# A two-block transformer on one core: the first matrix of each MLP as seven half-size products

## The chip, the cores and the metric

The kernel runs on one core of a Trainium2 chip. The metric is the device time of one execution in microseconds. TensorE multiplies matrices into PSUM, VectorE and ScalarE work elementwise, GpSimd does a few elementwise instructions, and SyncE (SP) issues all loads and stores.

## The reference

A sequence of 512 positions with 1024 features goes through three blocks: attention with an MLP, gated linear attention (GLA) with an MLP, and a hybrid mixer with a convolutional feed-forward. The part at hand is the MLP, which appears twice:

```python
def sq_relu_mlp(h, w_in, w_out):          # w_in 1024 x 4096, w_out 4096 x 1024
    return jnp.square(jax.nn.relu(h @ w_in)) @ w_out
...
for i in range(DEPTH):                    # DEPTH = 2
    ...
    h = h + sq_relu_mlp(rmsnorm(h, norm_mlp[i]), mlp_w_in[i], mlp_w_out[i])
```

All inputs are float32. The second reference block starts from a modulation, `mod = silu(c) @ w_ada + b_ada`, that depends on neither h nor x; the kernel computes it beside other work.

## The kernel before

Activations lie transposed: h is eight tiles of 128 features x 512 positions. A product keeps float32 precision with three matmuls in TensorE's faster float32r form: every operand x is split into a part xh rounded to float32r and a remainder xl = x - xh, and W x becomes Wh xh + Wh xl + Wl xh. ScalarE makes the rounded part (`hi`, line 456), VectorE the remainder (`lo`, line 459). `weights` (line 468) loads 128 x 1024 numbers of weights (512 KB) into a page w and splits them into wh and wl. `gemm` (line 478) then multiplies one such block into one PSUM bank: eight tiles k of 128 input features, three matmuls each, 24 matmuls of 512 columns.

`mlp` (line 803) first splits h times a gain into xs (`gained`, line 565). It goes through four groups g. In a group, eight blocks of the first matrix give eight tiles of 128 hidden features; each is multiplied with the norm's row rb after a maximum with 0 (VectorE), squared (ScalarE) and split into u. Then `residual` (line 758) runs the eight blocks of the second matrix that take this u, and VectorE adds each to h[n]. In the last group of the second MLP `halves` (line 972) does so with 256 columns at a time, so that the norm of the first 256 positions can start early. The modulation, `adaln` (line 764), is a generator: each `next(side)` in `mlp` lets it issue one more load of 512 KB (tile aw) and one multiply-add over 128 x 1024 on VectorE (tile acc).

`first` (line 990) opens the mixer and the feed-forward: it takes several blocks of weights at once, multiplies all of them with the first 256 positions, and then with the second, so that the second half of xs may come later. `ffn` (line 1284) calls it with seven blocks. `rope` (line 607) rotates queries and keys with four VectorE instructions; the attention calls it ten times, the mixer five times.

Nothing is issued in the order of the program text. `Plan` (line 95) records every instruction, then walks through them with a cost for each and, at each step, gives the engine that is free first its earliest instruction of the text that is ready. Tiles live in pages of five kinds (`PAGES`, line 421: bank, small, raw, half, full); an instruction that needs a page waits until one comes free, and it may not take a page that an earlier tile will need. `CAPS` limits some tags further. The result is one fixed order per engine.

Of the kernel before, what the change touches and what calls it, by code (L numbers as in the profile page):

```python
# [8 lines left out]
F = mybir.dt.float32  # L9
R = mybir.dt.float32r  # L10
I32 = mybir.dt.int32
U8 = mybir.dt.uint8
AF = mybir.ActivationFunctionType
OP = mybir.AluOpType
# [5 lines left out]
KT = 8  # L20
# [74 lines left out]
class Plan:  # L95
# [17 lines left out]
    def pages(self, kind, count):  # L113
        self.kinds[kind] = count
# [303 lines left out]
NCOL = _col_layout()  # L418


PAGES = {"bank": 8, "small": 96, "raw": 3, "half": 62, "full": 16}
CAPS = {"aw": 3, "acc": 2, "pth": 3, "ptl": 3, "wh": 4, "wl": 4, "qe": 3}
LASTING = ("cols", "ident", "hb", "g12", "mod", "w1024", "w256", "ones", "raw", "x2m", "fw", "ev", "blk", "part", "part", "bf", "k6", "fx", "fe", "rs")


class Net:
# [7 lines left out]
    def t(self, tag, cap, shape=(128, S), dt=F):  # L434
        size = math.prod(shape[1:]) * SIZE[dt]
        if tag in LASTING:
            return self.plan.lasting(tag, shape, dt)
        kind = "raw" if tag == "w" else next(k for k, b in (("small", 32), ("half", 2048), ("full", 4096)) if size <= b)
        return self.plan.tile(kind, tag, CAPS.get(tag), shape, dt)

    def g(self, shape=(128, S), dt=F):
# [8 lines left out]
    def bank(self, tag, shape=(128, S)):  # L450
        return self.plan.tile("bank", tag + "b", CAPS.get(tag + "b"), shape, F)

    def mm(self, out, lhsT, rhs, start, stop):
        self.nc.tensor.matmul(out, lhsT, rhs, start=start, stop=stop)

    def hi(self, out, x):
        self.nc.scalar.activation(out, x, AF.Copy)
# [30 lines left out]
    def gemm_nat(self, srcs, xs, n, bank="acc"):  # L488
        ws = []
        for src, kt in srcs:  # L490
            wh, wl = self.weights(src, (kt, n))
            ws += [(wh[:, k], wl[:, k]) for k in range(kt)]
        for i in range(4):
            ps = self.bank(bank)
            s = slice(i * 128, i * 128 + 128)
            for k, (xh, xl) in enumerate(xs):
                wh, wl = ws[k]
                self.mm(ps[:, :n], xh[:, s], wh, k == 0, False)
                self.mm(ps[:, :n], xh[:, s], wl, False, False)
                self.mm(ps[:, :n], xl[:, s], wh, False, k == len(xs) - 1)  # L500
            yield i, ps[:, :n]

    def rsqrt(self, x, n):
        nc = self.nc
# [102 lines left out]
    def rope(self, z, cs, sn, a=None):  # L607
        nc = self.nc
        sh, a = self.g(), self.g() if a is None else a
        nc.vector.stream_shuffle(sh, z, [j ^ 16 for j in range(32)])  # L610
        nc.vector.tensor_tensor(a, z, cs, op=OP.mult)
        nc.vector.tensor_tensor(sh, sh, sn, op=OP.mult)
        nc.vector.tensor_tensor(a, a, sh, op=OP.add)
        return a

    def keys(self, kn, e):
# [185 lines left out]

    def mlp(self, l, side=iter(()), after=None):
        nc, d, h = self.nc, self.d, self.h
        xs = self.gained(h, lambda k: self.col(f"nmlp{l}", k))
        rb = None
        for g in range(4):
            u = []
            for j in range(8):
                ps = self.gemm(d[f"w1_{l}"][g * 8 + j, 0], xs)  # L810
                if rb is None:
                    rb = self.row(self.rnorm(h, self.w1024)[0])
                next(side, None)
                t = self.g()
                nc.vector.scalar_tensor_tensor(t, ps, 0.0, rb, op0=OP.max, op1=OP.mult)
                nc.scalar.activation(t, t, AF.Square)
                u.append(self.split(t))
            if l == 0 or g < 3:
                self.residual(d[f"w2_{l}"], u, g, side)
            else:  # L820
                def evac(n, c, ps):
                    nc.vector.tensor_add(h[n][:, c], h[n][:, c], ps)
                    after(n, c)
                yield from self.halves(lambda n: d["w2_1"][n, 3], u, evac)

    def gla(self):
        nc, d, h = self.nc, self.d, self.h
# [183 lines left out]
    def mlp_norm2(self):  # L1011

        nc, h = self.nc, self.h
        gf = lambda k: self.col("fin", k)
        xs = [(self.t("xh", 8, dt=R), self.t("xl", 8, dt=R)) for _ in range(KT)]
        r1b, r12b = self.t("row", 2), self.t("row", 2)
        acc = [None]

        def squares(k, c):
            sq = self.big(dt=F)  # L1020
            nc.scalar.activation(sq[:, :256], h[k][:, c], AF.Square)
            nc.scalar.activation(sq[:, 256:], h[k][:, c], AF.Square, scale=gf(k))
            if k > 0:
                nc.vector.tensor_add(sq, acc[0], sq)
            acc[0] = sq

        for hf, c in self.mlp(1, after=squares):

            m, v = self.means(acc[0], self.w1024), self.small(4)
            nc.vector.tensor_scalar(v[:, :2], m[:, :2], EPS, None, op0=OP.add)  # L1030
            nc.vector.scalar_tensor_tensor(v[:, 2:], v[:, :2], EPS, m[:, 2:], op0=OP.mult, op1=OP.add)
            r = self.rsqrt(v, 4)
            self.row(r[:, 2:], r12b[:, c])
            self.row(r[:, :2], r1b[:, c])
        for hf in range(2):
            self.modulated(h, lambda k: self.g12[:, k:k + 1], 0, r12b, xs, slice(256 * hf, 256 * hf + 256))
        return xs, r1b
# [237 lines left out]
                (nc.vector if b == 2 else nc.gpsimd).tensor_tensor(m[n], m[n], x, op=OP.add)  # L1275

    def mlp0(self):
        side = self.adaln()
        for _ in self.mlp(0, side):
            pass  # L1280
        for _ in side:
            pass

    def ffn(self, xs):
        nc, d, h = self.nc, self.d, self.h
        ups = (0, 22, 1, 23, 2, 24, 3)
        pre = dict(zip(ups, self.first([d["wup"][j, 0] for j in ups], xs)))
        up = lambda j: pre.pop(j) if j in pre else self.gemm(d["wup"][j, 0], xs)
        y = [None] * KT
        for g, (j0, j1) in enumerate(((0, 8), (8, 16), (16, 22))):  # L1290
            u = []
            for j in range(j0, j1):
                a = up(j)
                c = self.g()
# [8 lines left out]
            for n in range(KT):  # L1303
                ps = self.gemm(d[f"wdn{g}"][n, 0], u)
# [5 lines left out]
        ps, sq, z = [None], [None], [None] * KT  # L1310
# [16 lines left out]
        for hf, c in self.halves(lambda n: d["wdn2"][n, 0], u, evac):  # L1327
            v = self.small(2)
            nc.vector.tensor_scalar(v, ps[0][:, :2], EPS, None, op0=OP.add)
            rb = self.bcast(self.rsqrt(v, 2))  # L1330
            for k in range(KT):
                x = y[k][:, c]
# [32 lines left out]
def _pack(w, kt):  # L1365
    k, n = w.shape
    return np.ascontiguousarray(w.reshape(k // (128 * kt), kt, 128, n // 128, 128).transpose(3, 0, 2, 1, 4)
                                ).reshape(n // 128, k // (128 * kt), 128, kt * 128)


def _nat(w, kt):
    k, n = w.shape
    return np.ascontiguousarray(w.reshape(k // (128 * kt), kt, 128, n).transpose(0, 2, 1, 3)).reshape(k // (128 * kt), 128, kt * n)


def _layout(a):
    a = {k: np.asarray(v) for k, v in a.items()}
    o = {}
# [3 lines left out]
    def put(name, v):  # L1382
        v = np.asarray(v).reshape(-1, 128).T
        cols[:, COLS[name]:COLS[name] + v.shape[1]] = v
# [11 lines left out]
    w = a["attn_w_qkv"][0]  # L1396
# [2 lines left out]
    o["wv"] = _nat(w[:, 1280:], 4)  # L1399
    o["wo"] = _pack(a["attn_w_o"][0], 8)  # L1400
    for l in range(2):
        o[f"w1_{l}"] = _pack(a["mlp_w_in"][l], 8)
        o[f"w2_{l}"] = _pack(a["mlp_w_out"][l], 8)
    w = a["gla_w_in"][0]
    o["wgq"] = _pack(w[:, :512], 8)
# [10 lines left out]
    j, c = np.arange(128)[:, None] % 64, np.arange(64)[None]  # L1416
# [63 lines left out]
```

## Time and profile before

| | |
|---|---|
| median of 3 runs | 1984.63 us (1984.07 to 1986.68) |
| profiled execution | 1984.77 us |
| its span | 1982.7 us |
| matmuls | 10389 |

The span runs from the first to the last instruction in the trace. Busy times are shares of it; matmuls overlap each other in the trace, so that a row's duration is longer than the time until the next one starts. In the trace all instructions carry the line of the recorder's `emit` (L352), so they are told apart by tile names and shapes.

### The profile page before, as it was taken

Reading aid. Unit: us, or ns where it says so; the run is one execution under the profiler, and the core shown is the slowest. Engines: PE = TensorE matmul, PEld = TensorE weight load, DVE = VectorE, ACT = ScalarE, POOL = GpSimd, SP = SyncE. Lnnn points to the kernel's source line nnn. Section 1 sums busy time; section 2 is a strip of 40 time slices with the busy share of each in tenths; the row PEclk is TensorE's granted clock in tenths of the full one; section 3 lists DMA queues with packets and bytes.
Section 4 is the critical chain, followed back from the end, with each engine's and each line's share of the span. In section 5 each row is a group of like instructions: output and inputs, shape, how many; then the busy total and the mean of one; then the engine's idle time right before and its main releaser. Section 6 shows DMA issues by size and latency. Waiting matters only on the chain.

```text
span 1982.7 us, 26560 instructions
## 1 busy us (share of the span) xinstructions
PE 1952.0 (98%) x10389; PEld 1654.6 (83%) x10389; DVE 1255.1 (63%) x2252; ACT 869.2 (44%) x1413; POOL 66.8 (3%) x110
## 2 busy tenths in 40 slices
PE   9899999999999999999999999999999999999997
PEld 8787788888889888888888899887888998888887
DVE  7999865746456677653434368899654685244346
ACT  6777642423346333442323255765443554233234
POOL 0000000000000001000000000100110000000001
PEclk9999999999999999999999999999999999999998
DMA  4012445745331222222323343231333423333322
GB/s 164 22 33 82 153 148 163 241 148 181 107 111 54 65 73 87 96 87 95 97 94 96 107 149 114 74 96 43 128 117 96 149 86 118 96 96 96 93 72 91
DMA packets 63628, 208.99 MB, mean 105 GB/s; under 512 B 7312, under 2 KB 10896, under 8 KB 63504
## 3 DMA queue, kind: packets, MB, share of 16 engines
q1 hardware_dynamic: 63504, 207.31, 32.7%
q8 instruction: 81, 1.33, 0.3%
q14 instruction: 43, 0.35, 0.1%
HBM read 203.08 MB, written 4.19 MB: 105 GB/s over the span
## 4 chain that ended last, share of the span: by engine, by line
PE 59%; DVE 1%; issue 0%; ACT 0%; POOL 0%
PE accb L352 50%; PE mb L352 3%; PE Sb L352 2%; PE ptb L352 2%; PE ob L352 1%; DVE big L352 1%; DVE c L352 0%; POOL ko L352 0%; ACT g L352 0%; ACT h L352 0%; DVE p L352 0%
## 5 line engine op out<-in xcount | busy, mean ns | idle before, releaser
L352 ACT ACTIVATE wh<-w 128x1024 fp32r<-128x1024 f32 (+2 forms) x337 | 346.3, 1030 | 730.7 <-PE accb L352 595.2
L352 DVE TENSOR_TENSOR wl<-w,wh 128x1024 fp32r<-128x1024 f32 (+2 forms) x336 | 399.3, 1190 | 274.9 <-ACT wh L352 195.4
L352 PE MATMUL accb<-big,wh 128*128 128x512 f32 (+1 forms) x2112 | 569.7, 357 | 0.0
L352 PE MATMUL accb<-xh,wh 128*128 128x512 f32 (+1 forms) x1344 | 524.5, 391 | 1.1 <-ACT wh L352 0.9
L352 PE MATMUL accb<-xl,wh 128*128 128x512 f32 (+1 forms) x1344 | 524.5, 390 | 0.0
L352 PE MATMUL accb<-xh,wl 128*128 128x512 f32 (+1 forms) x1344 | 523.4, 390 | 0.0
L352 PEld LDWEIGHTS accb<-big,wh 128*128 128x128 f32 x2112 | 373.1, 188 | 60.9 <-DVE big L352 0.2
L352 PE MATMUL accb<-big,wl 128*128 128x512 f32 (+1 forms) x1056 | 375.2, 356 | 0.0
L352 PEld LDWEIGHTS accb<-xh,wh 128*128 128x128 f32 x1344 | 253.2, 188 | 54.6 <-ACT wh L352 1.6
L352 PEld LDWEIGHTS accb<-xh,wl 128*128 128x128 f32 x1344 | 253.2, 188 | 53.0
L352 PEld LDWEIGHTS accb<-xl,wh 128*128 128x128 f32 x1344 | 253.3, 188 | 52.5 <-DVE xl L352 0.2
L352 PEld LDWEIGHTS accb<-big,wl 128*128 128x128 f32 x1056 | 198.7, 188 | 30.5
L352 DVE TENSOR_TENSOR h<-h,accb 128x512 f32<-128x512 f32 (+1 forms) x88 | 55.8, 635 | 109.4 <-PE accb L352 109.0
L352 DVE SCALAR_TENSOR_TENSOR g<-accb,row 128x512 f32<-128x512 f32 x64 | 44.0, 688 | 97.9 <-PE accb L352 93.6
L352 ACT ACTIVATE g<-g 128x512 f32<-128x512 f32 (+1 forms) x112 | 69.3, 629 | 74.9 <-DVE g L352 74.8
L352 DVE TENSOR_TENSOR big<-g,big 128x512 fp32r<-128x512 f32 (+2 forms) x124 | 81.8, 662 | 21.4 <-ACT big L352 21.1
L352 ACT ACTIVATE big<-g 128x512 fp32r<-128x512 f32 (+2 forms) x134 | 82.0, 613 | 29.9 <-DVE g L352 27.1
L352 DVE SCALAR_TENSOR_TENSOR acc<-aw,c,acc 128x1024 f32<-128x1024 f32 x42 | 53.8, 1281 | 24.8 <-DMA aw<-wada 24.6
L352 PE MATMUL ptb<-ident,p 128*128 128x128 f32 x376 | 61.2, 282 | 8.3 <-ACT p L352 4.6
L352 DVE TENSOR_TENSOR ptl<-ptb,pth 128x512 fp32r<-128x512 f32 (+2 forms) x112 | 64.4, 597 | 3.4 <-ACT pth L352 3.0
L352 PE MATMUL Sb<-big,q 128*128 128x512 f32 (+2 forms) x248 | 64.2, 379 | 2.1 <-ACT g L352 1.2
L352 PEld LDWEIGHTS ptb<-ident,p 128*128 128x128 f32 x376 | 45.6, 145 | 19.7 <-ACT p L352 12.1
(234 smaller groups left out, 2196.7 us busy)
## 6 DMA issues: line engine op xcount, KB each, us to landing
w<-w SPq DMA_DIRECT2D x136, 512.0 KB, 3.5
aw<-wada SPq DMA_DIRECT2D x48, 512.0 KB, 4.2
w<-wup SPq DMA_DIRECT2D x44, 512.0 KB, 3.5
w<-wzg SPq DMA_DIRECT2D x24, 512.0 KB, 3.5
w<-wout SPq DMA_DIRECT2D x16, 512.0 KB, 3.6
w<-wdn SPq DMA_DIRECT2D x16, 512.0 KB, 3.5
w<-wdn SPq DMA_DIRECT2D x16, 384.0 KB, 3.1
w<-wq SPq DMA_DIRECT2D x8, 512.0 KB, 4.5
```

The costliest lines, as they stand in the source:

```text
L352: getattr(getattr(self.nc, op.engine), op.name)(*map(real, op.args), **{k: real(v) for k, v in op.kwargs.items()})
```

## The change

The first matrix of each MLP is stored in quadrants of 256 x 512 (`_quads`). For a 2 x 2 split of weights (outputs by inputs) and of h (inputs by positions), `quad` forms seven products instead of eight, each of half the outputs, half the inputs and half the positions, in the Strassen-Winograd form. `spread` forms the sums of h once per MLP: seven right-hand sides with four tiles of 256 columns each, split like every operand. The sums of weights are three subtractions and an add of 128 x 1024 on VectorE per quad, before the split. Products 1, 6, 5 and 3 accumulate in one bank, with copies taken on ScalarE on the way (`kept`); products 7 and 4 share another, product 2 has its own. Two quads make a group's eight u tiles. The second matrix of group g - 1 is issued between the products of group g, one or two blocks at each `yield`; the first group has none between. The modulation now advances only at second-matrix blocks, so it reaches into the second MLP.

Pages change too: raw from 3 to 6 (it now holds the modulation's loads as well), half from 62 to 66, full from 16 to 11; the cap on acc goes. `first` in the feed-forward takes five blocks instead of seven. In `rope` two of the four VectorE instructions go to GpSimd.

```diff
-PAGES = {"bank": 8, "small": 96, "raw": 3, "half": 62, "full": 16}
-CAPS = {"aw": 3, "acc": 2, "pth": 3, "ptl": 3, "wh": 4, "wl": 4, "qe": 3}
+PAGES = {"bank": 8, "small": 96, "raw": 6, "half": 66, "full": 11}
+CAPS = {"aw": 2, "pth": 3, "ptl": 3, "wh": 4, "wl": 4, "qe": 3}
...
-        kind = "raw" if tag == "w" else next(k for k, b in (("small", 32), ("half", 2048), ("full", 4096)) if size <= b)
+        kind = "raw" if tag in ("w", "aw") else next(k for k, b in (("small", 32), ("half", 2048), ("full", 4096)) if size <= b)
...
+    def put(self, X, i, p, x):
+        xh, xl = self.pages(R), self.pages(R)
+        self.hi(xh, x)
+        self.lo(xl, x, xh)
+        X[p][2 * i:2 * i + 2] = [(xh[:, j], xl[:, j]) for j in range(2)]
+
+    def sums(self, X, i, B):
+
+        sub = lambda x, y: self.nc.vector.tensor_tensor(z := self.pages(), x, y, op=OP.subtract) or z
+        (b11, b12), (b21, b22) = B
+        t1, t3 = sub(b12, b11), sub(b22, b12)
+        t2 = sub(b22, t1)
+        t4 = sub(b21, t2)
+        for p, x in ((6, t2), (7, t3), (5, t1), (3, b22), (4, t4)):
+            self.put(X, i, p, x)
+
+    def spread(self, h, gain):
+
+        X, Bs = self.seven(), []
+        for i in range(2):
+            B = [[self.pages() for _ in range(2)] for _ in range(2)]
+            for r in range(2):
+                for c in range(2):
+                    for j in range(2):
+                        k = 4 * r + 2 * i + j
+                        self.nc.scalar.activation(B[r][c][:, j], h[k][:, c * 256:c * 256 + 256], AF.Copy, scale=gain(k))
+            Bs.append(B)
+            self.put(X, i, 1, B[0][0])
+        for i in range(2):
+            self.put(X, i, 2, Bs[i][1][0])
+        for i in range(2):
+            self.sums(X, i, Bs[i])
+        return X
+
+    def quad(self, src, X, sink):
+
+        nc = self.nc
+        A = {}
+        for r, i in ((0, 0), (0, 1), (1, 1), (1, 0)):
+            A[r, i] = self.t("w", 3, (128, 1024))
+            nc.sync.dma_start(A[r, i], src[2 * r + i])
+
+        def product(ps, x, p, start):
+            wh, wl = (self.t(a, 3, (128, 1024), R) for a in ("wh", "wl"))
+            self.hi(wh, x)
+            self.lo(wl, x, wh)
+            wh, wl = (a.rearrange("p (j k n) -> p j k n", j=2, k=4) for a in (wh, wl))
+            for n in range(8):
+                j, k = n // 2 % 2, n // 4 * 2 + n % 2
+                (xh, xl), o = X[p][k], ps[:, j]
+                self.mm(o, wh[:, j, k], xh, start and n == 0, False, skip_group_check=True)
+                self.mm(o, wh[:, j, k], xl, False, False, skip_group_check=True)
+                self.mm(o, wl[:, j, k], xh, False, n in (5, 7), skip_group_check=True)
+
+        def kept(ps):
+            z = self.pages()
+            nc.scalar.activation(z, ps, AF.Copy)
+            return z
+
+        sub = lambda z, x, y: nc.vector.tensor_tensor(z, x, y, op=OP.subtract)
+        a, b, c = (self.bank("acc", (128, 2, 256)) for _ in range(3))
+        product(a, A[0, 0], 1, True)
+        p1 = kept(a)
+        product(b, A[0, 1], 2, True)
+        sink(0, 0, b, p1)
+        yield
+        s1 = self.t("w", 3, (128, 1024))
+        nc.vector.tensor_add(s1, A[1, 0], A[1, 1])
+        sub(A[1, 0], A[0, 0], A[1, 0])
+        sub(A[0, 0], s1, A[0, 0])
+        product(a, A[0, 0], 6, False)
+        t6 = kept(a)
+        product(c, A[1, 0], 7, True)
+        yield
+        product(a, s1, 5, False)
+        t5 = kept(a)
+        sink(1, 1, c, t5)
+        yield
+        sub(A[0, 1], A[0, 1], A[0, 0])
+        product(a, A[0, 1], 3, False)
+        sink(0, 1, a, None)
+        product(c, A[1, 1], 4, False)
+        sink(1, 0, c, t6)
+        yield
...
-        nc.vector.tensor_tensor(sh, sh, sn, op=OP.mult)
-        nc.vector.tensor_tensor(a, a, sh, op=OP.add)
+        nc.gpsimd.tensor_tensor(sh, sh, sn, op=OP.mult)
+        nc.gpsimd.tensor_tensor(a, a, sh, op=OP.add)
...
     def mlp(self, l, side=iter(()), after=None):
         nc, d, h = self.nc, self.d, self.h
-        xs = self.gained(h, lambda k: self.col(f"nmlp{l}", k))
-        rb = None
+        X = self.spread(h, lambda k: self.col(f"nmlp{l}", k))
+        rb = self.row(self.rnorm(h, self.w1024)[0])
+
+        def hidden(g):
+
+            u = [None] * 8
+            for i in range(2):
+                T = [self.t("t", 3, (128, 2, 512)) for _ in range(2)]
+                left = [2, 2]
+
+                def sink(r, c, ps, x):
+                    t = T[r][:, :, c * 256:c * 256 + 256]
+                    if x is not None:
+                        nc.vector.tensor_add(t, ps, x)
+                        ps = t
+                    nc.vector.scalar_tensor_tensor(t, ps, 0.0, rb[:, None, c * 256:c * 256 + 256].to_broadcast([128, 2, 256]),
+                                                   op0=OP.max, op1=OP.mult)
+                    nc.scalar.activation(t, t, AF.Square)
+                    left[r] -= 1
+                    if not left[r]:
+                        for j in range(2):
+                            u[4 * r + 2 * i + j] = self.split(T[r][:, j])
+                for _ in self.quad(d[f"w1s_{l}"][g, i], X, sink):
+                    yield u
+
+        u = None
         for g in range(4):
...
+            out = [(w, n) for n, w in enumerate([d[f"w2_{l}"][n, g - 1] for n in range(KT)])] if g else []
+            for step, v in enumerate(hidden(g)):
+                for _ in range((1, 1, 2, 1, 1, 1, 1, 0)[step]):
+                    if out:
+                        w, n = out.pop(0)
+                        next(side, None)
+                        nc.vector.tensor_add(h[n], h[n], self.gemm(w, u))
+            u = v
+        if l == 0:
+            self.residual(d["w2_0"], u, 3, side)
...
-        for hf, c in self.mlp(1, after=squares):
+        for hf, c in self.mlp(1, self.modulation, squares):
...
-        ups = (0, 22, 1, 23, 2, 24, 3)
+        ups = (0, 22, 1, 23, 2)
```

## Rows read from the trace of the kernel before

**Rows 1.** The page: busy time of each engine, its share of the span, instructions.

```profile
PE 1952.0 (98%) x10389; PEld 1654.6 (83%) x10389; DVE 1255.1 (63%) x2252; ACT 869.2 (44%) x1413; POOL 66.8 (3%) x110
```

**Rows 2.** Busy time by stretch: PE, PEld, DVE, ACT, POOL, granted clock, DMA.

```profile
50.00:75.00 25.00, 21.90 (x121) 18.61 (x120) 24.65 (x80) 16.36 (x35) 0.62 (x1) 0.86 0.01 1
50.00:225.00 175.00, 163.17 (x985) 137.10 (x984) 168.13 (x423) 128.39 (x261) 8.58 (x8) 0.98 0.19 64
225.00:250.00 25.00, 25.00 (x110) 20.33 (x109) 17.77 (x24) 11.74 (x18) 0.00 (x0) 1.00 0.48 149
250.00:275.00 25.00, 25.00 (x118) 20.59 (x118) 14.55 (x27) 9.38 (x14) 0.00 (x0) 1.00 0.28 86
350.00:375.00 25.00, 25.00 (x109) 20.27 (x108) 21.19 (x23) 11.76 (x15) 0.00 (x0) 1.00 0.79 268
```

**Rows 3.** Timeline of TensorE: start us, duration us, instruction, count.

```profile
265.03 0.40 PE L352 MATMUL accb<-xh,wl 128*128 128x512 f32 x1
...
289.99 0.39 PE L352 MATMUL accb<-xh,wl 128*128 128x512 f32 x1
...
950.09 0.39 PE L352 MATMUL accb<-xl,wh 128*128 128x512 f32 x1
...
979.94 0.39 PE L352 MATMUL accb<-xh,wl 128*128 128x512 f32 x1
...
1164.06 0.40 PE L352 MATMUL accb<-big,wh 128*128 128x256 f32 x2
...
1183.90 0.28 PE L352 MATMUL accb<-big,wh 128*128 128x256 f32 x1
...
1192.19 0.36 PE L352 MATMUL accb<-big,wh 128*128 128x256 f32 x1
...
1207.89 0.28 PE L352 MATMUL accb<-xl,wh 128*128 128x256 f32 x1
```

**Rows 4.** Timeline of VectorE behind the attention and at the first MLP's front.

```profile
223.21 1.22 DVE L352 TENSOR_TENSOR wl<-w,wh 128x1024 fp32r<-128x1024 f32 x1
224.34 0.74 DVE L352 SCALAR_TENSOR_TENSOR xl<-h,cols,xh 128x512 fp32r<-128x512 f32 x1
...
249.79 0.69 DVE L352 TENSOR_TENSOR h<-h,accb 128x512 f32<-128x512 f32 x1 [2.13 <-PE accb L352]
```

**Rows 5.** Groups by shape: busy us, mean ns of one, idle before them.

```profile
L352 DVE TENSOR_TENSOR wl<-w,wh 128x1024 fp32r<-128x1024 f32 x306 | 374.9, 1226 | 255.4 <-ACT wh L352 176.1 <-issue 39.1 <-PE accb L352 37.6
L352 PEld LDWEIGHTS accb<-big,wh 128*128 128x128 f32 x2112 | 373.1, 188 | 60.9 <-DVE big L352 0.2 <-ACT big L352 0.2
L352 ACT ACTIVATE wh<-w 128x1024 fp32r<-128x1024 f32 x307 | 324.5, 1059 | 696.1 <-PE accb L352 567.9 <-DVE acc L352 47.4 <-issue 41.9
L352 DVE TENSOR_TENSOR big<-g,big 128x512 fp32r<-128x512 f32 x100 | 68.7, 688 | 21.2 <-ACT big L352 21.1
L352 DVE SCALAR_TENSOR_TENSOR acc<-aw,c,acc 128x1024 f32<-128x1024 f32 x42 | 53.8, 1281 | 24.8 <-DMA aw<-wada 24.6
L352 DVE SCALAR_TENSOR_TENSOR c<-c,c 128x4 f32<-128x4 f32 x60 | 9.7, 161 | 1.7
```

**Rows 6.** DMA issues: count, size, median us from issue to landing.

```profile
w<-w SPq DMA_DIRECT2D x136, 512.0 KB, 3.5
```

**Rows 7.** Timeline of TensorE and VectorE at the feed-forward's front.

```profile
1620.04 0.28 PE L352 MATMUL accb<-xh,wh 128*128 128x256 f32 x1
...
1617.70 1.27 DVE L352 SCALAR_TENSOR_TENSOR xl<-g,mod,xh 128x256 fp32r<-128x256 f32 x3
...
1622.32 0.89 DVE L352 SCALAR_TENSOR_TENSOR xl<-g,mod,xh 128x256 fp32r<-128x256 f32 x2 [0.18 <-ACT xh L352]
```

**Rows 8.** Timeline of GpSimd, and of VectorE beside GpSimd's last stretch.

```profile
1440.62 1.29 POOL L352 TENSOR_TENSOR h<-h,g 128x512 f32<-128x512 f32 x1 [5.83 <-DVE g L352]
...
1957.58 0.94 DVE L352 TENSOR_TENSOR big<-big,h 128x256 f32<-128x256 f32 x1
...
1960.68 0.41 DVE L352 TENSOR_TENSOR big<-big,h 128x256 f32<-128x256 f32 x1
```

More of the change, by code (lines that the diff above doesn't have):

```diff
@@ L451, in bank, with mm @@
         return self.plan.tile("bank", tag + "b", CAPS.get(tag + "b"), shape, F)
-    def mm(self, out, lhsT, rhs, start, stop):
-        self.nc.tensor.matmul(out, lhsT, rhs, start=start, stop=stop)
+    def mm(self, out, lhsT, rhs, start, stop, **k):
+        self.nc.tensor.matmul(out, lhsT, rhs, start=start, stop=stop, **k)
     def hi(self, out, x):
@@ L501, in gemm_nat, with pages, seven @@
             yield i, ps[:, :n]
+    def pages(self, dt=F):
+        return self.t("big" if dt == R else "g", 8, (128, 2, 256), dt)
+    def seven(self):
+        return {p: [None] * 4 for p in range(1, 8)}
+    def put(self, X, i, p, x):
[11 more added lines that the diff above has]
+            self.put(X, i, p, x)
@@ L804, in mlp @@
         nc, d, h = self.nc, self.d, self.h
-        xs = self.gained(h, lambda k: self.col(f"nmlp{l}", k))
-        rb = None
-        for g in range(4):
[L808 to L824, printed above, removed]
+        X = self.spread(h, lambda k: self.col(f"nmlp{l}", k))
@@ new lines, in mlp, with evac @@
+        u = None
+        for g in range(4):
+            out = [(w, n) for n, w in enumerate([d[f"w2_{l}"][n, g - 1] for n in range(KT)])] if g else []
[8 more added lines that the diff above has]
+            self.residual(d["w2_0"], u, 3, side)
+        else:
+            def evac(n, c, ps):
+                nc.vector.tensor_add(h[n][:, c], h[n][:, c], ps)
+                after(n, c)
+            yield from self.halves(lambda n: d["w2_1"][n, 3], u, evac)
@@ L1034, in mlp_norm2 @@
             self.row(r[:, :2], r1b[:, c])
+        for _ in self.modulation:
+            pass
         for hf in range(2):
@@ L1277, in mlp0 @@
     def mlp0(self):
[L1278 to L1281, printed above, removed]
+        self.modulation = self.adaln()
+        for _ in self.mlp(0, self.modulation):
             pass
@@ L1368, in _pack, with _quads @@
                                 ).reshape(n // 128, k // (128 * kt), 128, kt * 128)
+def _quads(w):
+    w = w.reshape(-1, 2, 4, 128, 2, 2, 2, 128)
+    return np.ascontiguousarray(w.transpose(0, 5, 4, 1, 3, 6, 2, 7)).reshape(-1, 2, 4, 128, 1024)
 def _nat(w, kt):
@@ L1401, in _layout @@
     for l in range(2):
-        o[f"w1_{l}"] = _pack(a["mlp_w_in"][l], 8)
+        o[f"w1s_{l}"] = np.stack([_quads(x)[0] for x in np.split(a["mlp_w_in"][l], 4, 1)])
         o[f"w2_{l}"] = _pack(a["mlp_w_out"][l], 8)
```

## The prediction

> **What bounds the kernel now.** I began with the page's busy times [rows 1]: TensorE is busy for 98% of the span, VectorE for 63%. A busy TensorE may still be a slow one, so I went to the busy time by stage next [rows 2]. [...] The attention of 50 to 225 us is the other kind: VectorE 168.1 of 175, TensorE 11.8 us idle. Last I took the distance of matmul starts from the timeline, since a row's own duration overlaps its neighbours [rows 3]. With 512 columns, 108 spacings between the first two rows give 231.1 ns and 130 between the next two 229.6 ns. With 256 columns, 168 spacings from 1164.06 us give 118.1 ns and 132 from 1192.19 us 118.9 ns; I take 118.5. Two halves cost 237 ns, 3% more than one whole.
>
> **The first matrices on TensorE.** Before, each MLP does 32 blocks of 24 matmuls, 768 of 512 columns: 768 x 0.2311 + 768 x 0.2296 = 353.8 us for both. After, one call of quad covers what four blocks did, with 7 products of 8 x 3 matmuls of 256 columns. That is 168 per quad, 8 quads per MLP, 2688 in all, x 0.1185 = 318.5 us, or 19.9 us per quad. Gain: **35.3 us**, between 34 and 36.4 by the two spacings. The second matrices keep their matmuls.
>
> [...]
>
> **VectorE in one quad.** A 128x1024 subtraction occupies 1.13 us (the start after it in [rows 4]; its row says 1.22, so 0.09 overlaps), and a 128x512 instruction 0.688 - 0.09 = 0.60 us [rows 5]. Before, four blocks needed 4 splits of weights, 4 maximum-multiplies and 4 splits of u: 4.5 + 4.8 = 9.3 us. A quad needs 7 splits and 4 sums of weights (11 x 1.13 = 12.4) and 3 adds, 4 maximum-multiplies and 4 splits of u (11 x 0.60 = 6.6): **19.0 us against 19.9 of TensorE**. ScalarE has 7 halves of weights and 11 smaller copies or squares; even 18 x 1.06 [rows 5] are 19.1, so it doesn't bind.
>
> In groups 1 to 3 four blocks of the second matrix lie between (4 x 24 x 0.231 = 22.2 us), with 4 x (1.13 + 0.60) = 6.9 us of VectorE. The modulation's 42 multiply-adds of 1.28 us and 12 reductions and transposes of about the same, now spread over both MLPs, add 69/14 = 4.9 us. So 30.8 against 42.1 us, 73%. Before, 21.19 of 25 (85%) went by with no TensorE wait [rows 2]. I take **+2** for these twelve quads; bounds 0 and 13 (one wait of 1.1 us per quad: an evacuation between two products chained in one bank, bounded by the 1.06 us of a ScalarE row twice as wide [rows 5]).
>
> **The first group of each MLP** has no second matrix in between, so the 0.9 us per quad is all the slack there is, and the sums over h come on top: 14 splits and 8 subtractions, 22 x 0.60 = 13.2 us, for the eight xl of before. The last h arrives at 250.4 us [rows 4]. What needs it: one split for product 2, three subtractions and four splits, 8 x 0.60 = 4.8 us, and the norm's last add and eleven small ones of 0.16 [rows 5], 2.4. Product 6 needs in addition two subtractions and an add on its weights and their split, 4.5 us. TensorE has products 1 and 2 to fill with, 5.7 us from 249.6. VectorE's worst order ends after 7.2 + 4.5 = 11.7 us, 7 us late once the 0.8 from 249.6 to 250.4 counts. But 225 to 250 us leaves 7.2 us of VectorE free [rows 2], and seven dropped xl return 7 x (0.74 - 0.09) = 4.6 [rows 4]; of these 11.8 the sums that don't need the last h take 8.4, and 3.4 go to product 6. That leaves some 4 us late. One more comes from the wait between products 5 and 3, which share a bank with only an evacuation between. 5 per MLP, **+10**; bounds 0 (all of it earlier) and 27 (7 late, two waits of 1.1, 4.2 of adds and splits left over, both MLPs).
>
> **Loads.** Bytes are the same. A quad holds four pages of weights and one sum out of six raw pages, shared now with the modulation's; a load that waits for a page holds back those behind it on SP's queue, the second matrix's too. Landing and the two halves of the split are 3.5 [rows 6] + 1.06 + 1.23 = 5.8 us; three pages come free by product 5, with products 3 and 4 and, from the second group on, at least one block of the second matrix to go (5.7 + 5.5 us). Nothing.
>
> **The front of the feed-forward** keeps 5 instead of 7 first blocks (wh and wl pages drop from 16 to 11). In before, the half that doesn't wait for the second half of xs ran until 1620.04 us; two blocks less end 2 x 24 x 0.1185 = 5.7 us earlier, at 1614.3. The first three xl of the second half are written from 1617.70 on, the last two from 1622.32 [rows 7]. So TensorE runs dry for some 3.8 us: **+4**, bounds 0 (other work found) and 7.5.
>
> **The rotation's two instructions on GpSimd.** Ten of the fifteen calls lie in the attention, where VectorE binds: 20 x 0.60 = 12 us less of it, at most the 11.8 us that TensorE idles. Against it, GpSimd takes 1.29 us each [rows 8], so eight queries come 8 x 1.4 = 11 us later if that is exposed; and a 256-wide add of VectorE beside GpSimd takes 0.94 where 0.41 is usual [rows 8], which eats 20 x 0.53 = 10.6. I take **-3**. [...]
>
> **Sum.** The profiled execution took 1984.77 us, 2.1 beside its span, 0.14 above the median of the three runs. 1984.8 - 35.3 + 10 + 2 + 4 - 3 = **1962.5 us**.
>
> **Rivals.** *The waits are hidden*: sums and page turns fit in the free time and the attention takes most of its idle back. 1984.8 - 35.3 + 2 + 2 - 8 = 1945.5. For it: 11.8 us free in 225 to 250; against: 19.0 beside 19.9.
> *VectorE paces every quad* (the other side): the 2.5 us that I give a quad of the first group recur in all 16, because the split of a weight sum waits behind adds and evacuations in VectorE's order. 1984.8 - 35.3 + 40 + 4 - 3 = 1990.5. It decides from (35.3 - 4 + 3)/16 = 2.1 us per quad. Against it: 73% busy in twelve of them.
> [...]
> *Weight loads pace the narrow matmuls.* At the 188 ns that a load's row shows [rows 5], 2688 of them take 505 us: +151, 2136. [...]
>
> **How the numbers follow.** Forecast 54%, hidden 20%, clock 13%, VectorE 12%, weight loads 1%. The forecast's own terms reach from 1950 to 1978. To leave out 2 in 10, I drop the last two on top and a third of the hidden case below: 1946 to 1982. Faster by over 0.2% (4 us, about what can be told from no change): 54 + 20 + 13 less 5 of their upper ends, 82%; within it 5%; slower 13%.
>
> **What would show it.** Right: 2688 matmuls of 256 columns some 118 to 119 ns apart; idle TensorE just behind each MLP's front with VectorE near full; none in groups 1 to 3; a gap of 3 to 4 us at the front of the feed-forward; less idle in the attention. Wrong: spacings above 132 ns (all gain gone), idle TensorE in every quad released by wl or by a bank's evacuation, or an attention that has grown by more than 5 us.

## The result and the profile after

The changed kernel takes **1966.28 us** (median of four runs, 1965.69 to 1967.98) against 1984.70 for the kernel before (median of four too): ratio 0.9907, 95% interval 0.989 to 0.9924. Its profiled execution took 1966.58 us with a span of 1964.8, against the forecast of 1962.5. So it is faster, and 4.1 us slower than forecast; but that small difference hides two larger errors that nearly cancel, and these are what the experiments are about.

The first matmul of each stage in TensorE's timeline (for the GLA the last one before it, 0.23 us earlier) cuts the span into six parts. This table is worked out in that way for both kernels (us):

| stage | before | after | difference |
|---|---|---|---|
| attention | 249.6 | 245.6 | -4.0 |
| first MLP | 357.2 | 340.4 | -16.8 |
| GLA | 241.1 | 248.9 | +7.8 |
| second MLP | 358.8 | 343.1 | -15.7 |
| mixer | 388.4 | 394.4 | +6.0 |
| feed-forward | 387.5 | 392.4 | +4.9 |

The MLPs give 32.5 us. Three stages whose arithmetic wasn't touched take 18.7 of them back, and of these the prediction had only the feed-forward's.

The page of the kernel after, busy times [rows 1]:

```profile
PE 1925.1 (98%) x11493; PEld 1685.3 (86%) x11493; DVE 1412.9 (72%) x2410; ACT 956.2 (49%) x1553; POOL 111.2 (6%) x140
```

VectorE has 158 us more work, and TensorE is as full as it was. Where it isn't is seen in the busy time by stretch of the kernel after (columns as in [rows 2]): the end of the attention, three stretches of the first MLP, the front of the GLA, the front of the feed-forward.

```profile
225.00:250.00 25.00, 25.00 (x127) 21.08 (x127) 21.21 (x31) 14.84 (x29) 0.00 (x0) 1.00 0.12 38
250.00:275.00 25.00, 25.00 (x212) 25.00 (x212) 24.62 (x40) 15.83 (x23) 0.00 (x0) 1.00 0.27 86
275.00:300.00 25.00, 25.00 (x189) 23.94 (x188) 24.31 (x28) 16.33 (x23) 0.00 (x0) 1.00 0.50 151
350.00:375.00 25.00, 25.00 (x166) 22.87 (x165) 19.27 (x21) 11.36 (x14) 0.00 (x0) 1.00 0.24 82
625.00:650.00 25.00, 20.72 (x151) 20.68 (x152) 17.38 (x31) 10.04 (x16) 0.00 (x0) 0.86 0.34 109
1575.00:1600.00 25.00, 22.34 (x177) 21.87 (x176) 18.71 (x59) 9.22 (x21) 0.00 (x0) 0.93 0.13 43
```

In the first group of the MLP (250 to 300 us) VectorE is at 24.3 to 24.6 of 25, as forecast, and yet TensorE loses nothing. It loses at 625 us, where nothing was expected. TensorE's and then VectorE's timeline of the kernel after at that place, the front of the GLA:

```profile
623.94 0.28 PE L352 MATMUL accb<-wh,xh 128*128 128x256 f32 x1
629.28 0.58 PE L352 MATMUL accb<-wl,xh 128*128 128x256 f32 x1 [5.06 <-DVE wl L352]
629.66 0.41 PE L352 MATMUL accb<-wh,xl 128*128 128x256 f32 x1
...
632.86 0.41 PE L352 MATMUL accb<-wh,xh 128*128 128x256 f32 x1
```

```profile
624.60 2.33 DVE L352 TENSOR_TENSOR_SCAN big<-mask,g 128x512 f32<-128x512 f32 x2
626.85 1.24 DVE L352 TENSOR_SCALAR big<-accb,c 128x256 f32<-128x256 f32 x3
628.01 3.48 DVE L352 TENSOR_TENSOR wl<-w,wh 128x1024 fp32r<-128x1024 f32 x3
```

TensorE waits 5.06 us for a remainder wl, which stands in VectorE's order behind the GLA's scans; three such splits come in a row there. At the same place of its GLA the kernel before has no gap:

```profile
645.80:670.80 25.00, 25.00 (x179) 23.46 (x178) 15.92 (x31) 8.20 (x11) 0.00 (x0) 1.00 0.27 85
```

And the wait costs more than itself: the 15 spacings from 629.66 to 632.86 us are 213 ns each, where 256 columns took 119.5 before the gap. The granted clock of the stretch is 0.86: 0.14 x 25 = 3.5 us of full clock. Not all of that is lost, for the clock fell while TensorE still waited, as two shorter stretches of the kernel after show:

```profile
628.10:629.28 1.18, 0.00 (x1) 0.01 (x1) 1.18 (x2) 0.06 (x1) 0.00 (x0) 0.52 0.00 0
629.28:635.00 5.72, 5.72 (x27) 5.72 (x28) 4.45 (x6) 0.00 (x0) 0.00 (x0) 0.50 0.75 238
```

In the second of them 26 spacings take 5.7 us instead of 26 x 0.1195 = 3.1. Wait and clock together are then 5.1 + 2.6 = 7.7 us, for a GLA that grew by 7.8.

The distance of matmuls in the first MLP, TensorE's timeline of the kernel after [rows 3]:

```profile
277.78 0.28 PE L352 MATMUL accb<-big,wl 128*128 128x256 f32 x1
...
289.97 0.28 PE L352 MATMUL accb<-big,wl 128*128 128x256 f32 x1
```

102 spacings in 12.19 us are 119.5 ns. The list of waits has no TensorE wait at all between 248 and 590 us or between 834 and 1178: neither MLP makes TensorE wait for anything.

### The profile page after: what moved, and what is told of

The parts are those of the page before. It is cut to its first block, busy times and chain, and to the rows that moved or that the text cites. A ratio compares the mean times of both kernels' runs of the same rounds, so it can differ in the third digit from the quotient of the medians.

```text
span 1964.8 us, 29011 instructions
## 1 busy us (share of the span) xinstructions
PE 1925.1 (98%) x11493; PEld 1685.3 (86%) x11493; DVE 1412.9 (72%) x2410; ACT 956.2 (49%) x1553; POOL 111.2 (6%) x140
## 4 chain that ended last, share of the span: by engine, by line
PE 58%; DVE 5%; issue 2%; ACT 1%; POOL 1%; DVEq 0%; POOLq 0%; ACTq 0%
PE accb L352 50%; PE mb L352 3%; DVE big L352 2%; PE ptb L352 2%; PE Sb L352 1%; PE ob L352 1%; DVE c L352 1%; DVE wl L352 1%; DVE q L352 0%; DVE p L352 0%; DVE g L352 0%; DVE ptl L352 0%; POOL kd L352 0%; POOL ko L352 0%; ACT wh L352 0%
## 5 line engine op out<-in xcount | busy, mean ns | idle before, releaser
L352 PE MATMUL accb<-big,wh 128*128 128x256 f32 (+1 forms) x3904 | 890.5, 323 | 0.0
L352 PEld LDWEIGHTS accb<-big,wh 128*128 128x128 f32 x3904 | 650.0, 189 | 62.0 <-DVE big L352 0.5
L352 PE MATMUL accb<-big,wl 128*128 128x256 f32 (+1 forms) x1952 | 627.4, 322 | 0.0
L352 PEld LDWEIGHTS accb<-big,wl 128*128 128x128 f32 x1952 | 369.0, 189 | 30.4
L352 PE MATMUL accb<-xh,wh 128*128 128x512 f32 (+1 forms) x848 | 329.8, 390 | 2.5 <-ACT xh L352 1.5
L352 PE MATMUL accb<-xh,wl 128*128 128x512 f32 (+1 forms) x848 | 328.8, 389 | 2.9 <-DVE wl L352 2.8
L352 PE MATMUL accb<-xl,wh 128*128 128x512 f32 (+1 forms) x848 | 329.6, 389 | 0.0
L352 PEld LDWEIGHTS accb<-xh,wl 128*128 128x128 f32 x848 | 160.5, 189 | 36.8 <-DVE wl L352 4.6
L352 PEld LDWEIGHTS accb<-xh,wh 128*128 128x128 f32 x848 | 160.6, 190 | 36.5 <-ACT xh L352 1.7
L352 PEld LDWEIGHTS accb<-xl,wh 128*128 128x128 f32 x848 | 160.3, 189 | 32.1 <-DVE xl L352 0.2
```

The source lines that it names most:

```text
L352: getattr(getattr(self.nc, op.engine), op.name)(*map(real, op.args), **{k: real(v) for k, v in op.kwargs.items()})
```

## The experiments

Each was timed beside the kernel before on the same chip, whose median was 1985.1 to 1985.2 us each time; the ratios are to that. Stage lengths come from each run's own trace, cut as in the table above.

**The page counts alone**, in the kernel before, without Strassen's products:

```diff
-PAGES = {"bank": 8, "small": 96, "raw": 3, "half": 62, "full": 16}
-CAPS = {"aw": 3, "acc": 2, "pth": 3, "ptl": 3, "wh": 4, "wl": 4, "qe": 3}
+PAGES = {"bank": 8, "small": 96, "raw": 6, "half": 66, "full": 11}
+CAPS = {"aw": 2, "pth": 3, "ptl": 3, "wh": 4, "wl": 4, "qe": 3}
...
-        kind = "raw" if tag == "w" else next(k for k, b in (("small", 32), ("half", 2048), ("full", 4096)) if size <= b)
+        kind = "raw" if tag in ("w", "aw") else next(k for k, b in (("small", 32), ("half", 2048), ("full", 4096)) if size <= b)
...
-        ups = (0, 22, 1, 23, 2, 24, 3)
+        ups = (0, 22, 1, 23, 2)
```

> The kernel before with the changed page counts (raw 6 with the modulation's loads in it, half 66, full 11) and five first blocks in the feed-forward, and nothing else changed. Theory (fewer full pages): the mixer lengthens by some 8 us and the feed-forward's front by 5, the GLA by 0 to 2 because the modulation still ends in the first MLP: near 1998 us. Rival (the rotation on GpSimd holds VectorE up in the mixer): the mixer stays, only the feed-forward's 5 us show: near 1990 us.

Measured 2005.85 us, ratio 1.0101 (1.0085 to 1.0116). The GLA is 249.2 with a TensorE wait of 5.2 us for wl at its front, the mixer 403.9 (+15.5), the feed-forward 393.3 (+5.8); the MLPs stay (356.0, 360.0), the attention is 7.5 shorter. That is 8 us above the expected 1998: the GLA, expected to grow by 0 to 2, grew by 8, and the mixer by twice the expected 8. So the losses outside the MLPs come without any Strassen product.

**The rotation alone**, in the kernel before:

```diff
-        nc.vector.tensor_tensor(sh, sh, sn, op=OP.mult)
-        nc.vector.tensor_tensor(a, a, sh, op=OP.add)
+        nc.gpsimd.tensor_tensor(sh, sh, sn, op=OP.mult)
+        nc.gpsimd.tensor_tensor(a, a, sh, op=OP.add)
```

> The kernel before with the rotation's two instructions on GpSimd and nothing else changed. Theory (fewer full pages cost the mixer its time): the attention shortens by some 4 us, the mixer stays: near 1981 us. Rival (GpSimd holds VectorE up): the mixer lengthens by up to 8 us and the attention's gain came from the modulation that no longer runs in its tail: near 1993 us.

Measured 1978.99 us, ratio 0.997 (0.996 to 0.9979): 6.2 us less, of which the attention's length shows 3.6 (246.0).

**The rotation back on VectorE**, in the changed kernel (the same four lines the other way):

> The changed kernel with the rotation back on VectorE. Theory: the attention gives its 4 us back, the mixer stays as long as in the changed kernel: near 1970 us. Rival: the mixer shortens by up to 8 us and the attention stays: near 1958 us.

Measured 1968.1 us, ratio 0.9912 (0.9897 to 0.9927), an interval that overlaps that of the change. In the traces the attention is 3.5 us shorter (242.1) and the mixer 8.2 longer (402.6), which neither the theory nor the rival had. By the time of the whole, what the rotation is worth in the changed kernel isn't told apart from nothing.

**The modulation earlier**: in the changed kernel, two of its steps at each block of a second matrix, so that it ends inside the first MLP, and not in the second. My guess at the time was that its pages, held through the GLA, made the GLA wait.

```diff
                         w, n = out.pop(0)
                         next(side, None)
+                        next(side, None)
```

> The changed kernel with two steps of the modulation at each second-matrix block of the first MLP, so that it ends there and its accumulator holds no full page through the GLA. Theory (that page costs the GLA's front its lead in weights): the wait of 5 us for wl and the lower clock behind it go, GLA 7 to 8 us shorter: near 1959 us. Rival (the lead is lost for another reason): the GLA stays and the sum stays at 1966 us, or grows by 1 to 3 if VectorE gets crowded in the first MLP.

Three executions took 1967.16, 1969.62 and 1976.1 us, ratio 0.9927 (0.9902 to 0.9952); a fourth took 2962.63 and is left out of the ratio. The GLA is 249.0, its 5.1 us wait is still there. That guess falls.

**Only the full pages**, in the kernel before: 11 instead of 16, and the five first blocks that go with them.

```diff
-PAGES = {"bank": 8, "small": 96, "raw": 3, "half": 62, "full": 16}
+PAGES = {"bank": 8, "small": 96, "raw": 3, "half": 62, "full": 11}
...
-        ups = (0, 22, 1, 23, 2, 24, 3)
+        ups = (0, 22, 1, 23, 2)
```

> The kernel before with 11 instead of 16 full pages and 5 instead of 7 first blocks in the feed-forward; its 3 raw and 62 half pages stay. Theory (the full pages alone cost the stages without Strassen products): GLA about 249 with the 5 us wait for a part of a weight at its front, mixer about 400, feed-forward about 393, MLPs 356 to 360, about 2004 in all. Rival (the first step's run with all page counts changed lost its time to the modulation's pages, now drawn from raw, or to the raw count): GLA stays near 241 and the mixer near 388, some 1989 with the feed-forward's 4.

Measured 2004.08 us, ratio 1.0096 (1.0079 to 1.0113); GLA 248.8, mixer 401.9, feed-forward 391.3. The waits by cause, first line, and the busy time by stretch of this run at the front of its GLA:

```profile
PE accb L352 <- DVE wl L352: 6.8, 5, 5.2
```

```profile
643.00:668.00 25.00, 19.76 (x150) 19.56 (x149) 17.96 (x31) 11.53 (x19) 0.00 (x0) 0.86 0.32 106
```

The same wait (5.2 the longest) and the same clock, 0.86. The full pages, which hold wh and wl, are the cause; the raw and half pages aren't needed for it.

**All large pages shared**: the changed kernel with raw and full as one kind of 17, and seven first blocks.

```diff
-PAGES = {"bank": 8, "small": 96, "raw": 6, "half": 66, "full": 11}
+PAGES = {"bank": 8, "small": 96, "half": 66, "full": 17}
-CAPS = {"aw": 2, "pth": 3, "ptl": 3, "wh": 4, "wl": 4, "qe": 3}
+CAPS = {"w": 6, "aw": 2, "pth": 3, "ptl": 3, "wh": 4, "wl": 4, "qe": 3}
...
-        kind = "raw" if tag in ("w", "aw") else next(k for k, b in (("small", 32), ("half", 2048), ("full", 4096)) if size <= b)
+        kind = next(k for k, b in (("small", 32), ("half", 2048), ("full", 4096)) if size <= b)
...
-        ups = (0, 22, 1, 23, 2)
+        ups = (0, 22, 1, 23, 2, 24, 3)
```

> The changed kernel, but the 6 raw and 11 full pages are one kind of 17 full pages that weights, their sums and all large tiles draw from, and the feed-forward begins with 7 first blocks again. Theory (a fixed share of 11 full pages is what costs the stages without Strassen products): the GLA loses its 5.2 us wait for a part of a weight and returns from 249 to about 241 us, the mixer from 394 to about 388, the feed-forward from 392 to about 388, the MLPs stay at 340 to 343: in all about 1947. Rival (the total of the pages binds, not how they are shared): no stage changes by more than 2 us, about 1966. A third outcome: a quad's five raw pages crowd out the pages of wh and wl in the MLPs, which then grow by several us.

Measured 2033.54 us, ratio 1.0246 (1.023 to 1.0262). The expected 1947 was wrong by 87 us, the third outcome holds: the MLPs grow to 367.8 and 380.0. The waits of TensorE in this run's first MLP:

```profile
PE accb L352 <- ACT wh L352: 10.3, 8, 4.2
PE accb L352 <- DVE wl L352: 4.2, 7, 1.4
```

The GLA stays at 248.0 with its 5.2 us wait, too, and as many splits lie ahead of its scans as in the changed kernel (120, counted from the start of the trace). My reading is that parts and sums, loaded ahead and not yet split, take the pages that the splits need; no run shows that by itself. Only the feed-forward, 386.2, is shorter, with seven first blocks again.

**Second matrices plainly after**, in the changed kernel: no plain blocks between the products of a quad.

```diff
-            out = [(w, n) for n, w in enumerate([d[f"w2_{l}"][n, g - 1] for n in range(KT)])] if g else []
-            for step, v in enumerate(hidden(g)):
-                for _ in range((1, 1, 2, 1, 1, 1, 1, 0)[step]):
-                    if out:
-                        w, n = out.pop(0)
-                        next(side, None)
-                        nc.vector.tensor_add(h[n], h[n], self.gemm(w, u))
+            for v in hidden(g):
+                pass
             u = v
+            if g < 3:
+                self.residual(d[f"w2_{l}"], u, g, side)
```

> The changed kernel with each group's second matrix plainly after its first matrix instead of between the products of the next group, so all 16 quads run without plain blocks between, as only the first group's four did. Theory (19.0 us of VectorE under 19.9 of TensorE hide also without plain blocks; the sums over h fit in the free time ahead): no wait in a quad, MLPs within 2 us of 340 and 343, total 1964 to 1970. Rival (a quad alone makes TensorE wait some 2.5 us, and the plain blocks in between hide it in groups 1 to 3): 12 more such quads, up to +30; each quad that is 0.8 us late, +10.

Measured 1972.31 us, ratio 0.9936 (0.9921 to 0.995). The MLPs are 342.2 and 346.2, 4.9 us more together; TensorE waits 1.1 us in the one and 2.2 in the other. The whole is 2 us above the expected range, so the theory holds in the main and not to the microsecond. A quad hides VectorE's work nearly by itself: 4.9 / 16 is 0.3 us per quad, where the rival wanted 2.5.

**Three more adds per quad**, in the changed kernel, a repetition of an add that is already there:

```diff
         nc.vector.tensor_add(s1, A[1, 0], A[1, 1])
+        nc.vector.tensor_add(s1, A[1, 0], A[1, 1])
+        nc.vector.tensor_add(s1, A[1, 0], A[1, 1])
+        nc.vector.tensor_add(s1, A[1, 0], A[1, 1])
```

> The changed kernel with the add of two weights' quarters done four times instead of once, so that a quad needs 19.0 + 3 x 1.13 = 22.4 us of VectorE beside 19.9 of TensorE. If my count of VectorE's work is right, the first group's two quads of each MLP must wait 2 x 2.5 = 5 us less what work ahead covers, and groups 1 to 3 (30.8 + 3.4 = 34.2 of 42.1 us) not at all: 2 to 5 us per MLP, 1970 to 1976. If the 19.0 was too high by 2.5 or more, nothing changes: 1966 to 1968. If groups 1 to 3 are nearer their bound than counted, 16 x 2 us and more: above 1990.

Measured 1985.07 us, ratio 1.0004 (0.9992 to 1.0015): the whole gain is gone. TensorE's waits in the first group of this run's first MLP, by its timeline, and the stretch that holds them:

```profile
276.99 0.51 PE L352 MATMUL accb<-big,wh 128*128 128x256 f32 x2 [1.16 <-ACT wh L352]
278.99 0.80 PE L352 MATMUL accb<-big,wh 128*128 128x256 f32 x2 [1.49 <-ACT wh L352]
281.19 0.58 PE L352 MATMUL accb<-big,wl 128*128 128x256 f32 x1 [1.41 <-DVE wl L352]
```

```profile
275.00:300.00 25.00, 20.95 (x156) 20.24 (x154) 20.96 (x24) 13.27 (x18) 0.00 (x0) 0.86 0.29 88
```

The waits, 4.1 us, lie in the expected 2 to 5: 2 x 3.4 us more work in the two quads, of which 2.7 were then free. The whole is 9 us above the expected 1970 to 1976. What the count left out is the clock, again 0.86 over the 25 us, and another 2.7 us of waits in groups 1 to 3. Of the lower clock some 2.0 us fell on work, an estimate: TensorE was busy for 4.61 us from 278.20 to 285.00, and its matmuls stood 213 ns apart from 281.57 to 284.77 instead of 119.5. The first MLP is 9.5 us longer than in the changed kernel, the second 10.7, in a profiled execution that took 1990.43 us, the slowest of ten and 5.4 above their median.

**Two halves without Strassen**, in the kernel before: 3072 matmuls of 256 columns in place of 1536 of 512.

```diff
-                ps = self.gemm(d[f"w1_{l}"][g * 8 + j, 0], xs)
+                ws = self.weights(d[f"w1_{l}"][g * 8 + j, 0], (KT, 128))
+                ps = self.bank("acc")
+                for c in (slice(0, 256), slice(256, 512)):
+                    self.block(ps[:, c], ws, xs, c)
```

> The kernel before with each block of the first matrices done as two runs of 24 matmuls of 256 columns into the two halves of its bank: the same arithmetic on TensorE at the changed kernel's width, without Strassen's products and sums: 3072 matmuls of 256 columns in place of 1536 of 512. Theory (a 256-column matmul with a weight load of its own takes 118.5 to 119.5 ns, 0.515 of the 230.4 of a whole): 3072 x 0.119 - 1536 x 0.2304 = +11.7 us, 9.9 to 13, about 1996. Rival (narrow matmuls are dearer where they alternate with weight loads of other pages, so that the gain of 32 us of the two MLPs is Strassen's 1/8 less such a loss): more than 13 us. A third outcome: no gain or loss within 3 us, and then the 2.4 us that each MLP falls short of 17.7 are waits.

Measured 1999.15 us, ratio 1.0073 (1.0058 to 1.0088). The first MLP is 5.9 us longer, second MLP and mixer together 6.9: (353.9 + 12.8) / 3072 = 119.4 ns per matmul, as in the changed kernel. In both a matmul of half the width costs 0.518 to 0.519 of a whole one. The 12.8 us of the stages lie in the theory's range, the 14.0 of the medians 1 us above it, where the rival begins; between the two this run decides to about 1 us only.

**Five first blocks alone**, in the kernel before:

```diff
-        ups = (0, 22, 1, 23, 2, 24, 3)
+        ups = (0, 22, 1, 23, 2)
```

> The kernel before with 5 instead of 7 first blocks at the front of the feed-forward and nothing else. Prediction's step: TensorE runs dry for some 3.8 us there, +4 (0 to 7.5), 1989. Rival (the feed-forward's 4.9 us come from the 11 full pages instead): nothing at the front, within 2 us of the kernel before.

Measured 1989.9 us, ratio 1.0021 (1.0011 to 1.0031); the feed-forward is 392.2, 4.7 more. The waits of TensorE in this run's first 42 us of that stage (the kernel before has none there), and the busy time of its first 25:

```profile
PE accb L352 <- ACT xh L352: 1.5, 1, 1.5
PE mb L352 <- DVE c L352: 1.3, 1, 1.3
```

```profile
1597.50:1622.50 25.00, 22.20 (x177) 21.75 (x177) 18.95 (x60) 9.00 (x23) 0.00 (x0) 0.95 0.14 44
```

2.8 us of waits and 0.05 x 25 = 1.3 of clock make most of the 4.7. The rival falls.

**13 full pages**, in the changed kernel: the same bytes, other shares, and six first blocks.

```diff
-PAGES = {"bank": 8, "small": 96, "raw": 6, "half": 66, "full": 11}
+PAGES = {"bank": 8, "small": 96, "raw": 5, "half": 64, "full": 13}
...
-        ups = (0, 22, 1, 23, 2)
+        ups = (0, 22, 1, 23, 2, 24)
```

> The changed kernel with 5 raw, 64 half and 13 full pages in place of 6, 66 and 11, and 6 first blocks in the feed-forward: the same bytes. Theory (the pages of the split weights are what the GLA, the mixer and the feed-forward lack): the GLA has one more split weight ready ahead of its four scans, loses the 5.1 us wait and goes from 249 to 242 to 244; the mixer goes from 394 to 390, the feed-forward from 392 to 390; the MLPs hold within 3 us: 1952 to 1958. Rival (a quad with four parts and a sum out of 5 raw pages has no page for the next load): a quad waits for wh, 5 to 30 us more in the MLPs, above 1966.

Measured **1951.38 us**, ratio 0.9834 (0.9819 to 0.9848), the best of the study with the next one. VectorE's timeline of this run behind the GLA's last scan, and the busy time by stretch at that front:

```profile
624.80 2.34 DVE L352 TENSOR_TENSOR_SCAN big<-mask,g 128x512 f32<-128x512 f32 x2
627.05 1.63 DVE L352 TENSOR_SCALAR big<-accb,c 128x256 f32<-128x256 f32 x4
628.60 2.35 DVE L352 TENSOR_TENSOR wl<-w,wh 128x1024 fp32r<-128x1024 f32 x2
```

```profile
617.30:642.30 25.00, 25.00 (x210) 24.93 (x210) 23.21 (x39) 17.16 (x25) 0.00 (x0) 1.00 0.28 89
```

Two splits stand in a row behind the scans and not three, since one more was done ahead of them: counted from the start of the trace, 121 splits of weights lie ahead of the GLA's first scan here and 120 in the changed kernel, 99 in the kernel before and 96 in the run with only the full pages cut. TensorE's wait is gone and the clock is 1.00. The GLA is 241.0 (7.9 less than in the changed kernel), the mixer 390.9 (-3.5), the feed-forward 387.3 (-5.1). The second MLP pays some of it back, 347.3 (+4.2, more than the expected 3), of which 2.3 are waits for split weights.

**13 full pages, the rotation shared**: VectorE keeps it in the attention, GpSimd in the mixer.

```diff
-            return self.rope(z, cs, sn), self.rsqrt(u, 8)
+            return self.rope(z, cs, sn, two=nc.vector), self.rsqrt(u, 8)
```

> The run with 13 full pages, and the rotation's two instructions on VectorE in the attention's ten calls, on GpSimd in the mixer's five. From the runs that moved the rotation: attention 242 instead of 245.6, mixer as with GpSimd: 3 to 4 us below the run with 13 full pages, the MLPs' and GLA's lengths unchanged. Rival (the 3.5 us of the attention were the clock's dips, and not the rotation): no difference of more than 1 us outside the dips.

Measured 1951.53 us, ratio 0.9835 (0.9819 to 0.985): no difference to the run before it, although its profiled attention is 240.7 and not 246.9. The attention's length in one trace is therefore no measure of a few us, and the rival holds for the whole. The run with the modulation earlier shows the same: up to the first MLP it issues the instructions of the changed kernel in the same order, and its attention took 251.0 us and not 245.6, in a profiled execution with a mean granted clock of 0.990 instead of 0.994.

## Why the prediction came out as it did

The terms of its sum, each with what it measured:

| term | forecast | measured | from |
|---|---|---|---|
| first matrices on TensorE | -35.3 | -32.5 | both MLPs' lengths |
| first group of each MLP | +10 | 0 | no wait in either |
| groups 1 to 3 | +2 | 0 | no wait in either |
| feed-forward's front | +4 | +4.9 | stage; +4.7 alone |
| attention | -3 | -4.0 | stage |
| GLA | none | +7.8 | stage |
| mixer | none | +6.0 | stage |

The forecasts sum to -22.3, the measured terms to -17.8 us, against -17.9 of the span.

- **The main term holds**, mis-sized by 2.8 us. It rests on matmuls alone setting the MLPs' time; TensorE waits for nothing there, neither in the kernel before (no wait in 250 to 606 us nor in 848 to 1206) nor after. I took 118.5 ns from [rows 3]; it measured 119.5 in the first MLP, and 2688 x 0.001 = 2.7. The products save one matmul in eight, 353.9 / 8 = 44.2 us, and the half width gives 2688 x (119.5 - 230.4 / 2) ns = 11.6 of it back. The run with two halves shows that loss by itself, 14.0 us by its median for 3072.
- **The first group's +10 is the step that failed among those named.** VectorE was as full as said (24.62 of 25), and no wait came of it. The mistake is in "VectorE's worst order": it set the two subtractions, the add and the split on product 6's weights behind the last h. Weights don't wait for h. VectorE's timeline of the kernel after:

```profile
221.68 1.22 DVE L352 TENSOR_TENSOR w<-w,w 128x1024 f32<-128x1024 f32 x1
...
231.72 1.23 DVE L352 TENSOR_TENSOR w<-w,w 128x1024 f32<-128x1024 f32 x1
...
245.83 0.69 DVE L352 TENSOR_TENSOR h<-h,accb 128x512 f32<-128x512 f32 x1 [1.60 <-PE accb L352]
246.44 1.22 DVE L352 TENSOR_TENSOR wl<-w,wh 128x1024 fp32r<-128x1024 f32 x1
```

All four sums of the first quad's weights were done by 232.95 us, 12.7 before the first product (245.63), in time that I had counted only from 225 us on. Behind the last h came one split of weights and nine instructions on h, done by 253.1 us, while products 1 and 2 ran until some 251.4 and 6 could begin with the half of its right-hand side that was ready. Nor did the wait of 1 us between products 5 and 3 come: TensorE's list of waits in the MLPs is empty.

- **The size of a quad's work, 19.0 us against 19.9, fits** the run with three more adds: with 19.0 TensorE doesn't wait, with 22.4 it does, and the slack of the first two quads comes out at 2.7 us where 2 x 0.9 was counted. The rival in which VectorE paces every quad falls with the run without plain blocks in between.
- **The feed-forward's front is right** in place, sign and size. Of its 4.7 us, 2.8 are waits, for ScalarE's xh and for a small VectorE result (c) and not for the xl that the prediction had there, and most of the rest is clock.
- **Loads at nothing held** for both MLPs: no TensorE wait behind them. With one raw and two half pages less (13 full pages) the second MLP is 4.2 us longer, so those weren't all idle.
- **The rotation's -3** is right in sign in the kernel before (-6.2). In the changed kernel its effect isn't told apart from nothing. What the attention's -4.0 consists of stays open: with the page counts alone the attention is 7.5 shorter, so the rotation added to that would have lengthened it by 3.5; the granted clock in 50 to 75 us is 1.00 in the kernel after and 0.86 before [rows 2]. The three traces with changed page counts and the rotation on VectorE there (242.1, 242.1, 240.7) lie below all six with it on GpSimd (245.6 to 251.0). But the length differs by 6 us between two kernels of equal median, and the times of the whole confirm none of it.
- **What was missing is a part that the prediction never priced**: 16 full pages became 11, and it followed that only into the feed-forward's first blocks. These pages set how many weights stand split ahead of a stretch in which VectorE is taken, and the GLA's scans are such a stretch (99 splits ahead of them with 16 full pages, 96 with 11). For the mixer's front that is argued and not shown. That 11 full pages cost the GLA 7.7 us and the mixer 13.5 by themselves is shown in the kernel before; 13 give 7.9 and 3.5 back. That the mixer loses 6.0 in the change but 13.5 to 15.5 without the rotation on GpSimd is borne out by the run with the rotation back, whose mixer is 402.6, 14.2 longer than before. Why is only argued: VectorE is near full there (24.88 of 25 in 1258 to 1283 us of the kernel after), so what GpSimd takes over may make room for splits; but in the kernel before it is as full (24.77 in 1355 to 1380 us) while TensorE loses nothing.
- **The clock**, with 13% of the chances, did fall, but not at the MLPs' fronts, where no gap came (1.00 over 250 to 300 us and over 834 to 884): it fell with the gap in the GLA (0.86 over 625 to 650 us) and at the feed-forward's front (0.93 over 1575 to 1600). In the GLA 3.5 us of clock weren't granted, and 2.6 of that fell on matmuls.
- **The rival of hidden waits** was right about the MLPs, where no wait came. Its 1945.5 leaves out the pages as the forecast does, and it gives the attention 8 us where 4.0 were measured.

The forecast's closeness is thus luck, owed to a cancellation: 12 us of waits that didn't come against 13.8 of pages that weren't counted.

## What to carry to other kernels

When a change pays for its buffers with another buffer's pages, price the stages that it doesn't touch: find the stretches in which the engine that fills those pages is taken, and count how many filled pages TensorE needs to get across. Work that doesn't depend on the last input isn't late when that input is late; take out of a "worst order" everything that is ready earlier before adding it up. And try the shares of a fixed memory as an experiment of its own: the same bytes in other shares, with the sixth first block that they allow, were worth 15 us here, where the change was worth 18.

## What the runs showed of the hardware

- A gap of 5 us in TensorE's work at the GLA's front, and 4 us in three pieces in the run with three more adds, each went with a granted clock of 0.86 over 25 us, and matmuls of 256 columns stood 213 ns apart right behind it instead of 119.5. The wait of 5.1 us cost 7.7 with the slow matmuls behind it, half its length again; part of the lower clock lay in the wait itself (0.52 in 628.10 to 629.28 us) and cost nothing.
- Four products in plain float32 of 128 columns each, eight rows of the trace, took 0.82 us in the kernel before, where one of 512 columns in the float32r form takes 0.23 [rows 3]:

```profile
40.16 1.05 PE L352 MATMUL mb<-ident,g 128*128 128x128 f32 x8
40.98 0.48 PE L352 MATMUL accb<-xh,wl 128*128 128x512 f32 x1
```

- The rotation's 20 instructions on GpSimd in the attention, on 128x512 tiles, took 1.27 to 2.28 us each (1.29 in [rows 8]), and a small VectorE instruction ended just behind one of them. Groups by shape of the kernel after (busy us, mean ns of one), then GpSimd's and VectorE's timeline in its attention:

```profile
L352 POOL TENSOR_TENSOR g<-g,g 128x512 f32<-128x512 f32 x13 | 22.5, 1737 | 17.8 <-DVE g L352 12.9 <-DVE c L352 4.7
```

```profile
54.12 1.80 POOL L352 TENSOR_TENSOR g<-g,tab 128x512 f32<-128x512 f32 x1
```

```profile
54.07 0.69 DVE L352 TENSOR_TENSOR big<-g,big 64x512 fp32r<-64x512 f32 x1
54.77 1.18 DVE L352 TENSOR_SCALAR c<-c 128x8 int32<-128x8 int32 x1
...
61.43 0.17 DVE L352 TENSOR_SCALAR c<-c 128x8 int32<-128x8 int32 x1
```

The small instruction on 128x8 took 1.18 us and ended at 55.95, just behind GpSimd's end at 55.92; the same one took 0.17 at 61.43. Not every instruction of VectorE is longer there: of those in the kernel after that lie for more than half beside such a GpSimd instruction, three of six splits of 128x1024 weights (w and wh are both in SBUF) took 2.28 to 2.31 us and the others 1.21 to 1.22, but all twelve of ptl from ptb and pth (ptb is in PSUM) took 0.67 to 0.69 us, as elsewhere (0.682 in the mean). These rows don't tell what parts the one kind from the other. As a whole the rotation on GpSimd gained 6.2 us in the kernel before.
